# Two-input work leaves GpSimd, and due times come from the last order: a transformer of two layers and a mixed-attention block on one core

## The chip, the core and the metric

The kernel runs on one core of a Trainium2 chip, in one launch. The time is the device time of an execution in microseconds (us); the time before is the median of three executions.

The engines and their names in the rows: PE is TensorE (matrix products and transposes; PEld its weight loads), DVE is VectorE, ACT is ScalarE, POOL is GpSimd, SP is the engine that issues the DMAs. Each engine works off its own queue in the order in which the program was written out, and waits on semaphores for the others.

## The reference

512 rows of x (1024 wide), one vector c, batch 1, all in float32. Two layers, then a second block:

```python
c_act = jax.nn.silu(c)
for layer in range(2):
    mod = c_act @ ada_w[layer] + ada_b[layer]
    sh1, sc1, g1, sh2, sc2, g2 = jnp.split(mod, 6, axis=-1)
    h = modulate(rms_norm(x, norm_g[layer, 0]), sh1, sc1)      # h * (1 + sc1) + sh1
    y = gmlp_mixer(h, ...) if layer == 0 else nsa_mixer(h, ...)
    x = x + g1[:, None, :] * rms_norm(y, norm_g[layer, 1])
    h = modulate(rms_norm(x, norm_g[layer, 2]), sh2, sc2)
    y = jnp.square(jax.nn.relu(h @ ff_w_in[layer])) @ ff_w_out[layer]
    x = x + g2[:, None, :] * rms_norm(y, norm_g[layer, 3])

def gmlp_mixer(h, w_in, ln_g, ln_b, w_s, b_s, w_out):
    u, v = jnp.split(jax.nn.gelu(h @ w_in), 2, axis=-1)
    v = layer_norm(v, ln_g, ln_b)        # then 8 groups of 128 columns, chunks of 128 rows
    mixed = jnp.einsum('gts,bcsgd->bctgd', tril(w_s), v) + b_s
    return (u * mixed) @ w_out
```

nsa_mixer is an attention of 16 heads over compressed, selected and windowed keys; the second block is a sum of stick-breaking and differential attention with a gate, and an output product.

## The kernel before

Every product is done in three products of halves: a float32 tile is split into a rounded upper half and the rest (hi and lo, in names h and l at the end), and TensorE adds hi x hi, hi x lo and lo x hi. So each weight tile (raw, 128 rows of 1024 columns, straight from a DMA) needs a copy that rounds (wh, or twh in the tail of a product) and a subtraction (wl or twl = raw - wh), and activations need the same (ah and al, tah and tal, hh and hl, vh and vl, pth and ptl, ...). `split` puts the subtraction on VectorE; `splitw` lets the planner choose for both parts; `flex` lets it choose VectorE or GpSimd for any two-input instruction.

The program isn't written in the order in which it runs. A recorder (`Rec`) notes every operation with its engine, or a list of engines, its dependences and buffers. `once` is a list scheduler: with a cost for each instruction it places operation after operation on the engine that comes free first, by priority among those that are ready, and gives buffers of limited pools (raw has 4). `dates` then goes through that order backwards, works out by when each operation is due, and makes this the priority of the operations off TensorE in the next pass; TensorE's operations keep the order of the program as their priority. `order` does this up to 12 times, keeps the pass whose planned end is the earliest, and the instructions go out in that order. All are issued from one line (L615), so the rows below are told apart by tile names.

The stages in time: the mixer of layer 1 (`gmlp`: transposes tp of the normed x, named hx before and xT after; v = vps, 30 to 79 us; u = fmps, 79 to 125; the group products pm; the output product acc, 139 to 205), its feed-forward (from 205 us), keys and values and the attention of layer 2 (inside 594 to 874 us, sA, sB, sC, tA to tC, po), its feed-forward, and the second block (inside 1310 to 1564 us).

The start: `cc` is c, then its silu, computed by way of e = exp(-c), a reciprocal and a product. Eight small diagonal tiles `diag` of it go into a product of TensorE (`cbp`) that spreads c over the partitions as the row `cb`. The modulation vectors are dot products on VectorE of the rows of ada_w with cb (written raw<-raw,cb), each with a vector from memory (vcol) added, as B and S; xT is scaled and shifted by B and S and split into hh and hl before vps can start. The reciprocal roots of x are made from squares on ScalarE (junkx), hv, rt and xrs.

The tail of the mixer: mx is made from pm, sg = sg * mx is u * mixed, tah and tal are its halves, and acc takes them with twh and twl, the halves of a_w_out, one slice k of 128 rows after the other.

Of the kernel before, what the change touches and what calls it, by code (L numbers as in the profile page):

```python
# [26 lines left out]
F32 = mybir.dt.float32  # L27
# [194 lines left out]
class Rec:  # L222
# [157 lines left out]
    def dates(self):  # L380

        heirs, last = {}, {}
        for o in self.ops:
            for b in o.bufs:
                if b.res and id(b) not in heirs:
                    heirs[id(b)] = None
                    k = b.pool, b.slot
                    if k in last:
                        heirs[last[k]] = o
                    last[k] = id(b)  # L390
        due, nxt = {}, None
        for o in reversed(self.ops):
            e, d = o.eng[0], o.eng[4]
            t = 1e12 if nxt is None else nxt if e == "pe" else 1e12
            for x in o.succ:
                t = min(t, due[x] - LAT[e][x.eng[0]])
            for b in o.bufs:
                h = heirs.get(id(b))
                if h is not None and h is not o:
                    t = min(t, due.get(h, 1e12) - 200)  # L400
            if o.eng[1] == "dma_start":
                d += 2460
            due[o] = t - d
            if e == "pe":
                nxt = due[o]
            else:
                o.prio = due[o]
# [263 lines left out]
class KB:  # L671
# [52 lines left out]
    def splitw(self, hi, lo, src):  # L724

        self.copyw(hi, src)
        self.flex("tensor_sub", lo, src, hi.bitcast(F32))

    def copyw(self, dst, src):

# [2 lines left out]

    def flex(self, m, *a, **k):

        self.R.add([("dve", m, a, k), ("pool", m, a, k)])

    def mac(self, out, x, s, y):

# [1336 lines left out]
```

## Time and profile before

| | |
|---|---|
| median of 3 executions | 1586.44 us (1580.53 to 1587.76) |
| the profiled execution | 1586.38 us |
| its span, first to last instruction | 1584.6 us |
| mean granted TensorE clock | 0.984 of full speed |
| busy share PE, DVE, ACT, POOL | 95%, 70%, 42%, 27% |
| HBM read, written | 205.33 MB, 6.34 MB |

How to read it: an engine's busy time counts its instructions from start to end, and what it stands still within an instruction is in it. A wait of TensorE is put down to the instruction of another engine that ended last before it. The granted clock is the share of TensorE's full speed that it was given in a stretch.

### The profile page before, as it was taken

How to read it: one execution, taken by the hardware profiler on the slowest of the kernel's cores; microseconds unless marked ns; L12 is line 12 of the kernel's file. 1: busy time of each engine (PE TensorE's matmuls, PEld its weight loads, DVE VectorE, ACT ScalarE, POOL GpSimd, SP SyncE). 2: the span in 40 equal slices, each digit the busy share in tenths (PEclk: the TensorE clock that was granted, in tenths of full speed). 3: DMA queues.
4: the chain of work that ended last, by engine and by line, in shares of the span. 5: the costliest groups of instructions: out<-in, count | busy, mean ns of one | idle time of the engine just before them, and what ended most of it. 6: DMA issues, size and time to landing. Idle time of an engine off the chain costs nothing. (4 is left out here: it accounts for less than half of the span.)

```text
span 1584.6 us, 20197 instructions
## 1 busy us (share of the span) xinstructions
PE 1508.1 (95%) x7410; PEld 1256.2 (79%) x7410; DVE 1103.8 (70%) x1957; ACT 667.5 (42%) x1443; POOL 425.7 (27%) x415
## 2 busy tenths in 40 slices
PE   4997899999999999999998999999999999999988
PEld 3786788888888889787876898888888888878777
DVE  6897686567874478777886684555674568688882
ACT  4441342222121456577786332222111337667680
POOL 4044100000111131475676000000242024243560
PEclk9998899999999999999998999999999999999999
DMA  9756189537841071300115256538512251112312
GB/s 347 238 186 173 30 292 288 187 133 276 340 154 40 28 249 54 112 1 28 28 31 170 67 200 182 172 111 252 180 45 67 89 181 54 54 54 55 80 47 100
DMA packets 151395, 212.98 MB, mean 134 GB/s; under 512 B 49536, under 2 KB 110208, under 8 KB 151296
## 3 DMA queue, kind: packets, MB, share of 16 engines
q1 hardware_dynamic: 151296, 211.69, 41.7%
q8 instruction: 58, 0.95, 0.3%
q14 instruction: 41, 0.34, 0.1%
HBM read 205.33 MB, written 6.34 MB: 134 GB/s over the span
## 5 line engine op out<-in xcount | busy, mean ns | idle before, releaser
L615 DVE TENSOR_TENSOR wl<-raw,wh 128x1024 fp32r<-128x1024 f32 x176 | 230.9, 1315 | 55.7 <-PE fmps L615 18.5
L615 DVE CAST wh<-raw 128x1024 fp32r<-128x1024 f32 x118 | 88.7, 752 | 123.5 <-PE fmps L615 96.7
L615 PE MATMUL acc<-wh,ah 128*128 128x512 f32 x432 | 168.9, 392 | 0.0
L615 PE MATMUL acc<-wl,ah 128*128 128x512 f32 x432 | 168.6, 392 | 0.0
L615 DVE SCALAR_TENSOR_TENSOR raw<-raw,cb 128x1024 f32<-128x1024 f32 x112 | 146.4, 1329 | 6.7 <-DMA raw<-in_kv_ada_w_dram 6.0
L615 PE MATMUL acc<-wh,al 128*128 128x512 f32 x432 | 134.5, 391 | 0.0
L615 ACT ACTIVATE r<-fmps 128x512 f32<-128x512 f32 x64 | 38.4, 599 | 210.7 <-PE fmps L615 210.7
L615 POOL TENSOR_TENSOR al<-hid,ah 128x512 fp32r<-128x512 f32 x10 | 16.9, 1694 | 401.2 <-ACT ah L615 388.8
L615 PE MATMUL acc<-twh,tah 128*128 128x512 f32 x272 | 107.2, 402 | 3.3 <-DVE twh L615 3.3
L615 PE MATMUL acc<-twl,tah 128*128 128x512 f32 x272 | 107.3, 403 | 3.1 <-DVE twl L615 3.1
L615 PE MATMUL fmps<-hfh,wl 128*128 128x512 f32 (+1 forms) x288 | 106.0, 368 | 2.3 <-DVE wl L615 2.3
L615 PE MATMUL fmps<-hfl,wh 128*128 128x512 f32 (+1 forms) x288 | 105.6, 367 | 0.0
L615 PE MATMUL fmps<-hfh,wh 128*128 128x512 f32 (+1 forms) x288 | 105.4, 368 | 0.1
L615 PE MATMUL fmps<-hf1l,wh 128*128 128x512 f32 (+1 forms) x288 | 105.2, 366 | 0.0
L615 PE MATMUL fmps<-hf1h,wl 128*128 128x512 f32 (+1 forms) x288 | 105.2, 366 | 0.0
L615 PE MATMUL fmps<-hf1h,wh 128*128 128x512 f32 (+1 forms) x288 | 104.8, 365 | 0.0
L615 ACT CAST ah<-hid 128x512 fp32r<-128x512 f32 x47 | 29.1, 619 | 157.7 <-PE acc L615 157.7
L615 PEld LDWEIGHTS acc<-wl,ah 128*128 128x128 f32 x432 | 81.6, 189 | 16.9
L615 PEld LDWEIGHTS acc<-wh,ah 128*128 128x128 f32 x432 | 81.4, 189 | 16.8
L615 PEld LDWEIGHTS acc<-wh,al 128*128 128x128 f32 x432 | 81.4, 189 | 16.7
L615 PE MATMUL acc<-twh,tal 128*128 128x512 f32 x272 | 88.2, 400 | 3.2 <-DVE tal L615 3.2
L615 ACT CAST wh<-raw 128x1024 fp32r<-128x1024 f32 x57 | 59.3, 1049 | 55.9 <-PE fmps L615 25.7
(561 smaller groups left out, 3995.0 us busy)
## 6 DMA issues: line engine op xcount, KB each, us to landing
raw<-in_ada_w_dram SPq DMA_DIRECT2D x40, 1024.0 KB, 7.5
raw<-in_ff_w_in_dram SPq DMA_DIRECT2D x32, 1024.0 KB, 10.5
raw<-in_ff_w_out_dram SPq DMA_DIRECT2D x32, 1024.0 KB, 5.0
raw<-in_w_in_dram SPq DMA_DIRECT2D x16, 1024.0 KB, 5.6
raw<-in_w_ada_dram SPq DMA_DIRECT2D x12, 1024.0 KB, 11.1
raw<-in_a_w_in_dram SPq DMA_DIRECT2D x8, 1024.0 KB, 8.6
raw<-in_ada_w_dram SPq DMA_DIRECT2D x16, 512.0 KB, 11.9
raw<-in_kv_ada_w_dram SPq DMA_DIRECT2D x8, 1024.0 KB, 14.2
```

Of the source, the lines that this page charges most:

```text
L615: getattr(real[e], m)(*a, **k)
```

## The change

Three lines. `dates` took as due time of a product that of the next product (nxt), from the end of the program backwards; now it takes the product's own end in the last order, its start plus its cost (the cost comes off again two lines on, so the product is due when it started). `splitw` no longer leaves the subtraction to the planner, and `flex` has VectorE alone as its engine. `copyw` (a copy on ScalarE, VectorE or GpSimd) stays, as do the instructions that are written for GpSimd (ws * tril, cP, cr, some copies).

```diff
--- before.py
+++ after.py
@@ -391,7 +391,7 @@
         due, nxt = {}, None
         for o in reversed(self.ops):
             e, d = o.eng[0], o.eng[4]
-            t = 1e12 if nxt is None else nxt if e == "pe" else 1e12
+            t = o.start + d if e == "pe" else 1e12
             for x in o.succ:
                 t = min(t, due[x] - LAT[e][x.eng[0]])
             for b in o.bufs:
@@ -724,7 +724,7 @@
     def splitw(self, hi, lo, src):
 
         self.copyw(hi, src)
-        self.flex("tensor_sub", lo, src, hi.bitcast(F32))
+        self.dve.tensor_sub(lo, src, hi.bitcast(F32))
 
     def copyw(self, dst, src):
 
@@ -733,7 +733,7 @@
 
     def flex(self, m, *a, **k):
 
-        self.R.add([("dve", m, a, k), ("pool", m, a, k)])
+        self.R.add([("dve", m, a, k)])
 
     def mac(self, out, x, s, y):
```

What it does to the order, first on SP, at the very start of the program, where x_79 and the like are the four row blocks of x. SP before:

```order
L615 DMA x_79<-in_x_dram 128x1024
L615 DMA x_87<-in_x_dram 128x1024
L615 DMA x_92<-in_x_dram 128x1024
L615 DMA x_94<-in_x_dram 128x1024
L615 DMA cc<-in_c_dram 128x8x1
L615 DMA raw<-in_a_w_in_dram 128x2x1024
L615 DMA raw_100<-in_ada_w_dram 128x1024 x2
```

The vector c is the fifth here, and the weights a_w_in come ahead of ada_w. SP after:

```order
L615 DMA cc<-in_c_dram 128x8x1
L615 DMA x_87<-in_x_dram 128x1024
L615 DMA x_92<-in_x_dram 128x1024
L615 DMA x_94<-in_x_dram 128x1024
L615 DMA x_96<-in_x_dram 128x1024
L615 DMA raw_98<-in_ada_w_dram 128x1024 x2
L615 DMA raw<-in_a_w_in_dram 128x2x1024
```

c is issued first now instead of fifth, and two rows of ada_w stand before the first weights.

The second place is VectorE just after the constants, up to the first dots. VectorE before:

```order
L615 TENSOR_SCALAR hv<-ss 128x4
L615 TENSOR_SCALAR e<-e 128x8
L615 RECIPROCAL e<-e 128x8
L615 TENSOR_TENSOR rt<-xrs 128x4
L615 TENSOR_TENSOR cc<-cc,e 128x8
L615 TENSOR_TENSOR rt<-rt,hv 128x4
L615 TENSOR_SCALAR diag<-ident,cc 128x128 x8
L615 SCALAR_TENSOR_TENSOR xrs<-rt,xrs 128x4
L615 TENSOR_SCALAR hx<-x_87,xrs 128x512
L615 COPY cb<-cbp 128x512
L615 SCALAR_TENSOR_TENSOR raw_100,S_186<-raw_100,cb 128x1024
L615 SCALAR_TENSOR_TENSOR raw_100,B_215<-raw_100,cb 128x1024
```

The roots (hv, rt) stand between the steps of cc here, and hv waits for all four squares of x. VectorE after:

```order
L615 TENSOR_SCALAR e<-e 128x8
L615 RECIPROCAL e<-e 128x8
L615 TENSOR_TENSOR cc<-cc,e 128x8
L615 TENSOR_SCALAR diag<-ident,cc 128x128 x8
L615 COPY cb<-cbp 128x512 x2
L615 TENSOR_SCALAR hv<-ss 128x4
L615 SCALAR_TENSOR_TENSOR raw_98,B_150<-raw_98,cb 128x1024
L615 TENSOR_TENSOR rt<-xrs 128x4
L615 TENSOR_TENSOR rt<-rt,hv 128x4
L615 SCALAR_TENSOR_TENSOR xrs<-rt,xrs 128x4
L615 TENSOR_SCALAR hx<-x_92,xrs 128x512
L615 TENSOR_SCALAR hx<-x_96,xrs 128x512
```

The eight diag and the two copies of cb stand ahead of all of the roots (hv, rt, xrs) now. ScalarE moves likewise: e comes ahead of the four squares junkx and not behind them, and a second load of its function table between them is gone.

The third place is the tail of the mixer, from pm to acc. GpSimd before:

```order
L615 TENSOR_TENSOR tal<-sg_722,tah 128x512
L615 TENSOR_TENSOR sg_722<-sg_722,mx 128x512 x2
L615 TENSOR_TENSOR tal<-sg_722,tah 128x512
L615 TENSOR_SCALAR twh<-raw 128x1024
L615 TENSOR_TENSOR sg_928<-sg_928,mx 128x512
L615 TENSOR_TENSOR twl<-raw,twh 128x1024
L615 TENSOR_SCALAR twh<-raw 128x1024
L615 TENSOR_TENSOR tal<-sg_722,tah 128x512
L615 TENSOR_TENSOR sg_928<-sg_928,mx 128x512
L615 TENSOR_TENSOR tal<-sg_928,tah 128x512
L615 TENSOR_TENSOR twl<-raw,twh 128x1024
```

GpSimd has two-input instructions of three kinds here (tal, sg, twl); after, only copies (twh) are left there. VectorE before:

```order
L615 TENSOR_TENSOR twl<-raw,twh 128x1024
L615 SCALAR_TENSOR_TENSOR mx<-pm,lngb,E 128x512
L615 TENSOR_TENSOR sg_722<-sg_722,mx 128x512
L615 TENSOR_TENSOR twl<-raw,twh 128x1024
L615 SCALAR_TENSOR_TENSOR raw,S_1000<-raw,cb 128x1024
L615 TENSOR_TENSOR tal<-sg_722,tah 128x512
L615 SCALAR_TENSOR_TENSOR raw,S_1000<-raw,cb 128x1024
L615 TENSOR_TENSOR twl<-raw,twh 128x1024
L615 TENSOR_TENSOR S_1000<-S_1000,vcol 128x8
L615 SCALAR_TENSOR_TENSOR raw,B_834<-raw,cb 128x1024
L615 TENSOR_TENSOR sg_928<-sg_928,mx 128x512
L615 SCALAR_TENSOR_TENSOR raw,B_834<-raw,cb 128x1024
```

Four dots (raw<-raw,cb) stand among the twl, tal and sg. VectorE after, from the fourth twl on:

```order
L615 TENSOR_TENSOR twl<-raw,twh 128x1024
L615 SCALAR_TENSOR_TENSOR mx<-pm,lngb,E 128x512
L615 TENSOR_TENSOR tal<-sg_711,tah 128x512
L615 TENSOR_TENSOR sg_711<-sg_711,mx 128x512
L615 TENSOR_TENSOR twl<-raw,twh 128x1024
L615 TENSOR_TENSOR tal<-sg_711,tah 128x512
L615 SCALAR_TENSOR_TENSOR mx<-pm,lngb,E 128x512
L615 TENSOR_TENSOR sg_931<-sg_931,mx 128x512
L615 TENSOR_TENSOR twl<-raw,twh 128x1024
```

The twl, tal and sg that GpSimd had stand on VectorE now, one mx, tal, sg and twl after the other, and the dots come ahead of this place or behind it, but for one.

## Rows read from the trace of the kernel before

**Rows 1.** Page, part 1: busy us (share of the span) xinstructions of each engine

```profile
PE 1508.1 (95%) x7410; PEld 1256.2 (79%) x7410; DVE 1103.8 (70%) x1957; ACT 667.5 (42%) x1443; POOL 425.7 (27%) x415
```

**Rows 2.** Busy time by stretches (window, length, engines with instructions, clock, DMA share, GB/s)

```profile
30.00:79.00 49.00, 47.09 (x193) 38.21 (x193) 40.02 (x77) 19.35 (x32) 6.20 (x4) 0.93 0.82 273
139.00:160.00 21.00, 14.32 (x39) 10.20 (x40) 21.00 (x20) 6.95 (x10) 15.42 (x8) 0.67 0.34 118
160.00:205.00 45.00, 40.00 (x179) 32.65 (x178) 32.76 (x59) 16.35 (x41) 7.47 (x3) 0.92 0.32 77
240.00:540.00 300.00, 300.00 (x1330) 248.48 (x1329) 189.02 (x258) 69.28 (x115) 25.65 (x19) 1.00 0.54 189
594.00:874.00 280.00, 264.38 (x1507) 217.93 (x1507) 219.68 (x543) 192.00 (x483) 157.21 (x205) 0.98 0.22 60
1310.00:1564.00 254.00, 239.10 (x1212) 200.61 (x1211) 198.91 (x352) 164.32 (x369) 110.01 (x93) 0.99 0.20 58
```

**Rows 3.** TensorE's waits, whole run: us in total, times, longest us

```profile
PE cbp L615 <- DVE diag L615: 18.1, 1, 18.1
...
PE acc L615 <- DVE twh L615: 3.3, 1, 3.3
```

**Rows 4.** Timelines of four engines, 4 to 30 us: start us, us, instruction

```profile
4.42 1.06 ACT L615 ACTIVATE junkx<-x 128x1024 f32<-128x1024 f32 x1 [2.40 <-DMA x<-in_x_dram]
...
11.28 0.21 ACT L615 ACTIVATE e<-cc 128x8 f32<-128x8 f32 x1
...
12.99 5.85 DVE L615 TENSOR_SCALAR diag<-ident,cc 128x128 f32<-128x128 f32 x8
...
13.14 4.64 POOL L615 TENSOR_TENSOR wl<-raw,wh 128x1024 fp32r<-128x1024 f32 x2
...
29.73 1.12 PE L615 MATMUL vps<-wh,hh 128*128 128x512 f32 x2 [2.59 <-ACT hh L615]
```

**Rows 5.** Tile cc: durations ns min/median/max of the diag made from it

```profile
L615 DVE TENSOR_SCALAR diag<-ident,cc x8: 273/275/2380, 13.0 to 18.6; 128x128 f32<-128x128 f32 x8
```

**Rows 6.** Timelines of VectorE, GpSimd and TensorE, 138 to 206 us

```profile
138.57 0.69 DVE L615 CAST twh<-raw 128x1024 fp32r<-128x1024 f32 x1 [5.72 <-DMA raw<-in_a_w_out_dram]
...
146.33 3.41 DVE L615 SCALAR_TENSOR_TENSOR raw<-raw,cb 128x1024 f32<-128x1024 f32 x1
...
156.70 1.21 DVE L615 SCALAR_TENSOR_TENSOR raw<-raw,cb 128x1024 f32<-128x1024 f32 x1
...
159.59 0.68 DVE L615 TENSOR_TENSOR tal<-sg,tah 128x512 fp32r<-128x512 f32 x1
...
145.29 3.37 POOL L615 TENSOR_TENSOR twl<-raw,twh 128x1024 fp32r<-128x1024 f32 x1
...
205.12 0.28 PE L615 MATMUL fmps<-hfh,wh 128*128 128x256 f32 x1
```

**Rows 7.** VectorE's groups from 139 to 160 us: xcount, busy us, mean ns

```profile
L615 DVE SCALAR_TENSOR_TENSOR raw<-raw,cb 128x1024 f32<-128x1024 f32 x4 | 8.1, 2035 | 0.0
L615 DVE TENSOR_TENSOR twl<-raw,twh 128x1024 fp32r<-128x1024 f32 x3 | 6.6, 2215 | 0.0
L615 DVE TENSOR_TENSOR tal<-sg,tah 128x512 fp32r<-128x512 f32 x2 | 2.2, 1095 | 0.0
```

**Rows 8.** GpSimd's groups, whole run

```profile
L615 POOL TENSOR_TENSOR wl<-raw,wh 128x1024 fp32r<-128x1024 f32 x18 | 46.6, 2589 | 17.1 <-DVE wh L615 11.1 <-PE dpo L615 2.2 <-issue 2.1
...
L615 POOL TENSOR_TENSOR al<-hid,ah 128x512 fp32r<-128x512 f32 x10 | 16.9, 1694 | 401.2 <-ACT ah L615 388.8 <-PE acc L615 7.8 <-DVE ah L615 4.7
```

**Rows 9.** VectorE's groups, whole run

```profile
L615 DVE TENSOR_TENSOR tal<-hid,tah 128x512 fp32r<-128x512 f32 x7 | 11.2, 1624 | 0.0
```

**Rows 10.** GpSimd's wl from 0 to 240, 594 to 874, 1310 to 1564 us

```profile
L615 POOL TENSOR_TENSOR wl<-raw,wh 128x1024 fp32r<-128x1024 f32 x5 | 13.5, 2700 | 8.7 <-DVE wh L615 8.6
...
L615 POOL TENSOR_TENSOR wl<-raw,wh 128x1024 fp32r<-128x1024 f32 x3 | 8.0, 2663 | 5.6 <-DVE wh L615 2.5 <-issue 2.1 <-PE po L615 1.0
...
L615 POOL TENSOR_TENSOR wl<-raw,wh 128x1024 fp32r<-128x1024 f32 x9 | 21.8, 2418 | 2.8 <-PE dpo L615 2.2 <-ACT wh L615 0.2
```

## The prediction

> **What bounds the kernel now.** I read the page first, then busy time by stretches, then TensorE's waits, then the timelines of the places that came out of these. On the page [rows 1] TensorE is busy 1508.1 of 1584.6 us; VectorE has 70%, GpSimd 27%. So the work on TensorE is the floor, and only the stretches where it runs dry can give anything.
>
> The stretches [rows 2] say which these are. From 240 to 540 us TensorE is busy 300.00 of 300 us with 1330 instructions at a granted clock of 1.00, which is 300/1330 = 0.226 us for each. I use that as the price of a 512-column product without a wait. There, and in the other feed-forward, work that VectorE gains or loses lies under products: VectorE has 189 of the 300 us. Losses stand in four places. (1) The first product starts at 18.11 us; its wait is the longest of the kernel [rows 3]. (2) From 139 to 160 us only 39 products run in 21 us (39 x 0.226 = 8.8, so 12.2 lost), VectorE is busy in all 21.00 us, the granted clock is 0.67 (between the two levels of 1.2 and 2.4 GHz), and from 160 to 205 another 45 - 179 x 0.226 = 4.5 us go: 16.7 us together, and the waits of acc for twh [rows 3] and for other split halves are in it. (3) From 594 to 874 us (the attention of layer 2) TensorE is idle 280 - 264.4 = 15.6 us. (4) From 1310 to 1564 us 254 - 239.1 = 14.9 us.
>
> What makes place 1 late [rows 4]: the sigmoid of c stands on ScalarE behind four squares of x and a second table load, so e starts at 11.28 us. Then VectorE has eight diag, 275 ns at the median; the longest takes 2380 ns [rows 5], and the eight 5.85 us, while GpSimd works on two wl from 13.14 us on. They end at 12.99 + 5.85 = 18.8 instead of 12.99 + 8 x 0.275 = 15.2. The reciprocal roots and, through the column cb, the first product of the mixer (vps, 29.73 us) wait behind that.
>
> What makes place 2 late [rows 6]: beside GpSimd's twl of 3.37 us VectorE's dot takes 3.41 us; alone, ten us later, the same form takes 1.21, and a tal 0.68.
>
> **The price of a two-input instruction.** GpSimd takes 2589 ns on a mean for a wl of 128x1024 [rows 8], where VectorE alone takes 1.21 us for that size; at 128x512 it is 1694 against 0.68. And GpSimd's time isn't free for VectorE: the seven tal that it does now among GpSimd's work take 1624 ns on a mean [rows 9]. VectorE's 139 to 160 us by groups [rows 7] give 4 x (2035 - 1210) + 3 x (2215 - 1210) + 2 x (1095 - 680) = 7.1 us, and with two small ones 8.5 us, above the undisturbed times. The same subtraction over VectorE's rows of a stretch gives some 40 us before 240 us, 13 in place 3 and 41 in place 4.
>
> The Trainium skill ("SBUF — State Buffer", section "SBUF: two separate sides") has VectorE and GpSimd share a port pair that the first one holds for its whole instruction while the other stands still. The 2380 ns of a 275 ns diag agree. The same notes ("Perfetto Trace Analysis", section "Optimizing Scalar/DVE Operations") speak on the other side as well: with VectorE saturated, giving work to ScalarE or even GpSimd may make sense. By that advice the stretches where VectorE is fullest would become slower; rival C works that out from rows, and the durations just given are why I think less of it.
>
> **Edit by edit.** Edits two and three (splitw, flex) give all these instructions to VectorE. GpSimd keeps one-input copies, which still disturb, the mask products and cP, cr; its instructions fall from 420 to 342, VectorE's rise by 102 (the order's counts). By stretch, from the counts on GpSimd (its wl in each stretch: [rows 10]) and VectorE's undisturbed durations:
>
> - To 222 us: 5 wl and 2 twl at 1.21, 5 vg, 5 sg, 4 tal, 3 vl at 0.68: 8.5 + 11.6 = +20 us. Against it stand the 40 us of delay; I let 8 of them stay, for copies. VectorE's net: -12.
> - Place 3: 3 wl, 3 twl, 8 instructions of 128x512, 4 ptc of 0.41 us: 7.3 + 5.4 + 1.6 = +14. Of 13 us of delay perhaps 10 go. Net +4; TensorE is dry there in 6% of the time and VectorE busy 78%, so about half shows: **+2** (bounds -6, no delay left and the shorter latencies shown, and +14, all work shown and no delay gone).
> - Place 4: 9 wl, 2 twl, 16 of 128x512, 9 smaller: 13.3 + 10.9 + 3.7 = +28; of 41 us of delay some 35 go. Net -7, half of it shown: **-4** (bounds -15, all the idle time, and +12).
> - The feed-forwards take the rest (6 of 128x1024, 19 al and tal: 7.3 + 12.9 = 20 us) and hide it under saturated products: 0. Were that cover gone, these 20 us would show.
>
> Edit one (the due time of a product is now its own start in the last order, with no chain backwards without gaps) costs no instruction. It reorders, and three things of it can be seen in the order. SP issues c first, before x. ScalarE does e before the squares, with one table load. VectorE does the diag before the roots. So place 1: c takes the place in which x landed by 4.42 us (start of the first square, [rows 4]); from e's start to the first diag there are 12.99 - 11.28 = 1.7 us, with two instructions of the roots between, and 8 x 0.275 = 2.2 us follow: diag ends at 4.4 + 1.7 + 2.2 = 8.3 us, and 3 us later if c should land that much after x did. From the first product to vps the trace has 29.73 - 18.11 = 11.6 us; I keep it, though the vector vcol and the first ada rows have to land too: vps at 20 to 22 us. **-9** (bounds -4, if the landings hold it, and -10).
>
> Then 30 to 79 us: 193 x 0.226 = 43.6 of 49 us; VectorE 40.02 busy. What edits two and three add here is about what they take away; 0. From there to 125 us the products run without a gap, and the +3.4 of vg and +2 of vl stand against some 7 us of delay; 0.
>
> Place 2: GpSimd's twl, tal and sg become 2 x 1.21 + 4 x 0.68 + 5 x 0.68 = 8.5 us on VectorE, and the 8.5 us of delay above and some 5 more up to 170 us go. The order helps more: of the four dots among the twl only one is left there, the others (3 x 1.21, now 2.04 each) come behind. VectorE then has mx, sg, tal and twl of 0.74 + 0.68 + 0.68 + 1.21 = 3.3 us for each slice k, TensorE 24 products of 0.226 = 5.4. So after the first slice it can keep ahead, and the waits shrink to the first. I take **-9** of the 16.7 (bounds -2 and -14; a start below the full clock stays).
>
> **The sum**: -9 - 9 + 2 - 4 = -20 us. The profiled run took 1586.38 us (span 1584.6), as good as the median of 1586.44, so: **1566 us**.
>
> **Rivals.**
> - A, the head start does not last: the weights of a_w_out land late. VectorE's twh waited 5.72 us for that landing [rows 6]. If buffers come free no sooner, -9 of place 1 shrinks to -2, and place 2 gives the half: -2 - 4 + 2 - 4 = 1578. For it: the DMA engines are 0.82 busy from 30 to 79 us; against it: 0.34 from 139 to 160 [rows 2].
> - B, no change to speak of: the delay by GpSimd's two-input instructions is only moved to its copies, which the new order makes more of (twh 7 to 13, pth and ptc too), and the new due times hold the old gaps: place 1 alone gains, and +14 of place 3 meets it: -9 + 9 = 1586.
> - C, VectorE becomes the bound, on the other side: in place 3, where it is 78% busy on the mean, heads run in a chain of mask, exponential, split and product, and every added instruction that stands ahead of a ptl delays TensorE. It decides if VectorE passes about 90% from 680 to 840 us; then +14 and place 4's +12 show, less 10 for the start: 1602.
> - D, the delays matter more than I counted: places 3 and 4 lose all their excess, -6 and -15, and the first stage -23: 1542.
>
> **Chances.** Forecast 0.52, A 0.16, B 0.11, C 0.11, D 0.10. Half a per cent is 8 us, about what a measurement of this kernel can tell from no change; the lines are 1578.5 and 1594. Faster: all of the forecast but 0.02, half of A, all of D: 0.68, and 0.04 from B; 0.72. Slower: C and a little of B, 0.11; the rest, 0.17, is the same. The range drops the ends of C and D: 1548 to 1588; the forecast's own is 1556 to 1577.
>
> **What would show it.** GpSimd has no wl, twl, al or tal; the first product stands at 8 to 11 us and vps at 20 to 22; no diag is above 0.4 us; from 139 us on no dot takes over 2 us, and acc's waits fall below 3 us together; the first layer's feed-forward (fmps from hfh) begins near 187 instead of 205.12 us [rows 6]; VectorE's count rises by 102 and its busy time by less than the 20 + 14 + 28 + 20 = 82 us that were given to it. I am wrong if vps is not earlier than 26 us, if TensorE's busy share falls in 680 to 840 us, or if copies on GpSimd delay VectorE as much as wl did.

## The result, and the profile after

The changed kernel takes 1558.47 us on the median of four executions (1554.99 to 1562.43), beside 1585.66 us of the kernel before (1580.53 to 1587.76): a ratio of 0.9834, interval 0.980 to 0.987. In a second set of runs it was 0.9808 (0.9795 to 0.9821), 30 us less. The forecast was 1566 us, 20 less than before, and a range of 1548 to 1588. The profiled execution took 1554.99 us with a span of 1553.2 us, 31 us less than the profile before; it was the fastest of the four, so the differences by stage below add up to a few us more than the medians give (31 against 27).

The page of the changed kernel, busy time by engine, to hold against [rows 1]:

```profile
PE 1499.9 (97%) x7410; PEld 1252.3 (81%) x7410; DVE 1086.9 (70%) x2059; ACT 651.0 (42%) x1419; POOL 261.7 (17%) x337
```

TensorE's busy share is 97% instead of 95%. It stands still for 53.3 us (1553.2 - 1499.9) where it stood still for 76.5, and its 7410 instructions are busy for 8.2 us less. So 23 of the 31 us are waits, and 8 are the same products in less time; the granted clock below bears on those. VectorE has 2059 instructions instead of 1957, the 102 that the order said, and is busy 17 us *less* (1086.9 against 1103.8), though it took over work of 82 us. GpSimd fell by 164 us.

TensorE's longest waits, whole run (us in total, times, longest), to hold against [rows 3]:

```profile
PE tp L615 <- DVE rt L615: 7.3, 1, 7.3
PE cbp L615 <- DVE diag L615: 4.8, 1, 4.8
PE wst L615 <- POOL ws L615: 4.7, 1, 4.7
PE tp L615 <- ACT hx L615: 4.6, 1, 4.6
PE fmps L615 <- ACT vg L615: 4.4, 1, 4.4
```

The 18.1 us in front of cbp are 4.8. The waits of acc, 9.6 us together before, have left one of 0.7. Two of these five are new, wst and fmps, both before the mixer's group products; they are spoken of below.

The diag, to hold against [rows 5], and tal beside its row of before [rows 9], both on VectorE:

```profile
L615 DVE TENSOR_SCALAR diag<-ident,cc x8: 281/281/288, 3.9 to 5.3; 128x128 f32<-128x128 f32 x8
```

```profile
L615 DVE TENSOR_TENSOR tal<-hid,tah 128x512 fp32r<-128x512 f32 x16 | 12.4, 814 | 0.0
```

No diag is held up any more (288 ns at the most against 2380), and sixteen tal take 814 ns on a mean where seven took 1624.

Some of TensorE's instructions on its timeline (start us, us), at fixed points of the first 125 us, with the wait in brackets:

```profile
4.85 2.07 PE L615 MATMUL cbp<-diag,shared 128*128 128x512 f32 x2 [4.85 <-DVE diag L615]
...
19.31 0.71 PE L615 MATMUL vps<-wh,hh 128*128 128x512 f32 x2
...
67.69 0.79 PE L615 MATMUL fmps<-hh,wh 128*128 128x512 f32 x1 [4.40 <-ACT vg L615]
...
88.43 1.12 PE L615 MATMUL wst<-ident,ws 128*128 128x128 f32 x4 [4.66 <-POOL ws L615]
...
122.46 0.33 PE L615 MATMUL pm<-wsT,vh 128*128 128x128 f32 x2
```

The first product is at 4.85 us, vps at 19.31 instead of 29.73 [rows 4]: 10.4 us earlier. But pm starts at 122.46, and before at 125.3: of the 10.4 us only 2.8 are left there, lost at the waits of 63.3 to 67.7 and of 83.8 to 88.4.

Stretches of the changed kernel (columns as in [rows 2]):

```profile
20.00:40.00 20.00, 20.00 (x89) 16.12 (x88) 19.78 (x40) 8.72 (x11) 1.07 (x1) 1.00 1.02 410
60.00:80.00 20.00, 15.60 (x60) 12.41 (x59) 14.91 (x45) 13.29 (x35) 2.13 (x2) 0.83 1.02 327
80.00:100.00 20.00, 15.34 (x63) 12.28 (x62) 9.86 (x32) 6.73 (x11) 3.59 (x3) 0.83 0.84 198
133.00:154.00 21.00, 20.26 (x89) 15.89 (x89) 20.26 (x27) 6.38 (x9) 3.67 (x3) 1.00 0.27 101
154.00:190.00 36.00, 28.71 (x130) 23.81 (x129) 24.78 (x60) 13.96 (x37) 1.55 (x1) 0.91 0.42 103
240.00:520.00 280.00, 280.00 (x1241) 231.95 (x1240) 178.46 (x251) 59.68 (x100) 8.55 (x8) 1.00 0.53 191
576.00:849.00 273.00, 261.01 (x1505) 216.26 (x1504) 226.06 (x562) 191.04 (x482) 129.33 (x190) 0.98 0.23 62
1285.00:1533.00 248.00, 239.20 (x1213) 201.03 (x1212) 194.50 (x383) 159.63 (x359) 67.38 (x76) 0.99 0.19 59
```

From 20 to 40 us the DMA engines are full (1.02). After the two waits the granted clock is 0.83 in both stretches, where products without a wait have 1.00; a part of each loss is a product at the lower of the two levels. In the tail of the mixer, now 133 to 154, 89 products run in 21 us where 39 did, at a clock of 1.00, and the half after it is shorter. The windows of the attention and of the second block are set so that they hold the same products as in [rows 2] within two (1505 and 1507, 1213 and 1212): 273 us instead of 280, and 248 instead of 254. From 240 to 520 us nothing shows: 1241 instructions in 280 us, 0.226 us each, as before.

The places at which an instruction starts, in the traces, and the lead on the kernel before:

| | before | changed | lead |
|---|---|---|---|
| first product (cbp) | 18.1 | 4.8 | 13.3 |
| first vps | 29.7 | 19.3 | 10.4 |
| first pm | 125.3 | 122.5 | 2.8 |
| eighth hfl (VectorE; all transposes for the first feed-forward done) | 222.5 | 202.6 | 20.0 |
| R (VectorE; keys and values of layer 2) | 594.3 | 576.1 | 18.2 |
| first hf1l (VectorE; attention done) | 897.1 | 872.3 | 24.7 |
| eighth h2l (VectorE; second block begins) | 1281.5 | 1255.4 | 26.1 |
| last fy (VectorE) | 1581.1 | 1549.7 | 31.4 |

The first product of the feed-forward (fmps from hfh) starts at 190.58 us, before at 205.12.

The second profiled execution of the same kernel runs within 0.6 us of the first up to 771 us and is 4.1 us behind by 853. The attention, from R to the first hf1l, in the kernel before, the changed kernel and its second profile (columns as in [rows 2]):

```profile
594.27:897.07 302.80, 287.18 (x1611) 236.81 (x1610) 230.37 (x563) 197.40 (x498) 157.21 (x205) 0.98 0.21 59
576.12:872.33 296.21, 284.22 (x1611) 235.53 (x1610) 235.58 (x581) 195.81 (x496) 129.33 (x190) 0.98 0.22 60
576.67:876.43 299.76, 288.31 (x1611) 238.60 (x1610) 236.01 (x580) 195.93 (x496) 129.32 (x190) 0.97 0.22 60
```

TensorE stands still for 15.6 us before and for 12.0 and 11.5 us in the two profiles after. The second of these is longer although it waits less: the same 1611 instructions are busy for 4.1 us more, at a granted clock of 0.97 instead of 0.98. So a length in the attention is known to about 4 us only, its waits much better.

### The profile page after: what moved, and what is told of

Same layout as the page of the kernel before. It is cut to its first block, busy times and chain, and to the rows that moved or that the text cites. A ratio compares the mean times of both kernels' runs of the same rounds, so it can differ in the third digit from the quotient of the medians.

```text
span 1553.2 us, 20146 instructions
## 1 busy us (share of the span) xinstructions
PE 1499.9 (97%) x7410; PEld 1252.3 (81%) x7410; DVE 1086.9 (70%) x2059; ACT 651.0 (42%) x1419; POOL 261.7 (17%) x337
## 3 DMA queue, kind: packets, MB, share of 16 engines
HBM read 205.33 MB, written 6.34 MB: 136 GB/s over the span
## 4 chain that ended last, share of the span: by engine, by line
PE 79%; DVE 11%; ACT 3%; DMA 3%; issue 2%; POOL 1%; SPq 1%; POOLq 0%; DVEq 0%; ACTq 0%
PE acc L615 29%; PE fmps L615 27%; PE tmc L615 3%; PE qps L615 3%; PE po L615 3%; PE sgps L615 2%; DVE wl L615 2%; DVE raw L615 1%; PE vps L615 1%; PE tmb L615 1%; PE sB L615 1%; DVE ptl L615 1%; PE tp L615 1%; PE sA L615 1%; PE kps L615 1%
## 5 line engine op out<-in xcount | busy, mean ns | idle before, releaser
L615 DVE TENSOR_TENSOR wl<-raw,wh 128x1024 fp32r<-128x1024 f32 x194 | 239.4, 1236 | 39.4 <-PE fmps L615 18.5
L615 DVE CAST wh<-raw 128x1024 fp32r<-128x1024 f32 x119 | 83.6, 703 | 120.3 <-PE fmps L615 94.3
L615 DVE SCALAR_TENSOR_TENSOR raw<-raw,cb 128x1024 f32<-128x1024 f32 x112 | 133.9, 1222 | 11.9 <-DMA raw<-in_kv_ada_w_dram 7.2
L615 ACT CAST ah<-hid 128x512 fp32r<-128x512 f32 x48 | 29.7, 620 | 159.4 <-PE acc L615 159.4
L615 POOL TENSOR_SCALAR tah<-hid 128x512 fp32r<-128x512 f32 x5 | 5.3, 1076 | 472.5 <-DMA raw<-in_ff_w_out_dram 208.5
L615 ACT CAST wh<-raw 128x1024 fp32r<-128x1024 f32 x52 | 54.5, 1049 | 55.2 <-PE fmps L615 32.0
## 6 DMA issues: line engine op xcount, KB each, us to landing
raw<-in_ff_w_in_dram SPq DMA_DIRECT2D x32, 1024.0 KB, 10.4
raw<-in_w_ada_dram SPq DMA_DIRECT2D x12, 1024.0 KB, 11.8
```

The costliest lines, as they stand in the source:

```text
L615: getattr(real[e], m)(*a, **k)
```

## The experiments

"VectorE's delay" below is a sum over its instructions in a trace: what each one took beyond the lower quartile of the times of its operation and shape in that trace, where it took more. For the kernel before it is 36 us before 240 us, 14 from 594 to 874 and 40 from 1310 to 1564; for the changed kernel 9, 7 and 13 in the same windows. Over the whole run 129 became 43.

Where these delays lie says who makes them. In the kernel before 142 instructions are held up by over 0.1 us, 116 us together, and every one of them overlaps an instruction on GpSimd: 87 a two-input one (96.5 us), 55 one-input ones alone (19.8 us). In the changed kernel it is 29 us in 78 instructions, and 76 of them (28.8 us) overlap one-input instructions alone.

**The due times alone.**

```diff
-            t = 1e12 if nxt is None else nxt if e == "pe" else 1e12
+            t = o.start + d if e == "pe" else 1e12
```

> The kernel before with the due-time line alone; VectorE and GpSimd share the two-input work as before, by a new plan. Theory of the forecast (the port between VectorE and GpSimd costs most, the due times only bring c and the diag ahead): the first product near 5 us and vps near 20, but the tail of the mixer and the attention stay as slow as before, so about 1586 - 10 = 1576 us (0.994). Rival (the better order does it all, the engine matters little): about 1558, as the full change. Second rival (the start's gain is caught by the next wait): 1582 to 1586.

Measured: 1577.06 us, 0.9938 (0.9914 to 0.9962). The total is the one that the theory of the forecast gave, and the first rival falls. The stages are not as the theory had them: vps has a lead of 9.9 us and pm of 4.4, so half of it is caught by the next waits; the tail (8.2 at the eighth hfl), which was to stay as slow as before, gains 3.8 us in the new plan, the attention 3.1 (6.4 at R, 9.4 at the first hf1l), and the end has 11.6. That the sum fits is in part luck. The tal among GpSimd's work are as slow as in [rows 9]:

```profile
L615 DVE TENSOR_TENSOR tal<-hid,tah 128x512 fp32r<-128x512 f32 x8 | 11.9, 1507 | 0.0
```

**The engines alone.**

```diff
-        self.flex("tensor_sub", lo, src, hi.bitcast(F32))
+        self.dve.tensor_sub(lo, src, hi.bitcast(F32))
...
-        self.R.add([("dve", m, a, k), ("pool", m, a, k)])
+        self.R.add([("dve", m, a, k)])
```

> The kernel before with the two engine edits alone, due times as before. Theory of the forecast: the start stays late (c behind x, first product at about 16, since no wl delays a diag), the tail of the mixer, the attention and the second block gain what the port gave back: 1586 - 17 = 1569 us (0.989). Rival (the order does it all): 1586. If both edits are needed for each other, both single runs stay above 1575.

Measured: 1554.41 us, 0.9787 (0.9765 to 0.9809). More than forecast, and all that the full change gives. c is late here as in the kernel before (first product at 13.8, vps at 23.3, a lead of 6.4), pm is at 125.5 with no lead at all, and yet the eighth hfl has 17.2 us and the end 30.7. So the early c is not needed for the gain.

**The same order, other engine.**

```diff
+        for o in self.ops:
+            if o.eng[0] == "pool" and len(o.alts) == 2 and o.alts[0][1] == o.alts[1][1]:
+                o.eng = o.alts[0]
         self.ops.sort(key=lambda o: (o.start, o.seq))
```

> The order of the kernel before, row for row, but every two-input instruction that the plan gave to GpSimd is issued on VectorE at its place in that order. Nothing else moves. If the port is the cause, the change of engine alone gains even in an order that was not made for it: 1586 - 12 = 1574 us, most of it before 240 us and after 1310. If it is the work on VectorE that counts and the gain comes of the new order, this is slower than before: 82 us more work in a plan that has no room for it, 1590 to 1600.

Measured: 1575.24 us, 0.9921 (0.9902 to 0.994). The change of engine alone gains 12.6 us in an order that wasn't made for it; the engines with an order made for them (1554.41 in the same set) gain 20.8 more. Where the 12.6 lie is the more telling part: the lead is 5.5 us at vps, 7.3 at pm, 10.9 at the eighth hfl and at R, 4.5 at hf1l, and 10.7 at the end. In the second block this kernel gains 6.2 us. The attention is 6.4 us longer (columns as in [rows 2]):

```profile
583.35:892.57 309.22, 293.40 (x1611) 241.32 (x1610) 237.29 (x581) 198.11 (x498) 126.42 (x187) 0.96 0.21 58
```

But TensorE doesn't wait more there, 15.8 us against 15.6 before: its products are busy for 6.2 us more, at a granted clock of 0.96 instead of 0.98. The added work doesn't show as waits even in this order. The clock alone moves this stretch by 4 us between two executions of one kernel, so whether the order has a part in the 6.4 us stays open.

From pm to the first product of the feed-forward (fmps from hfh) the kernel before, this run and the changed kernel take:

```profile
125.25:205.12 79.87, 65.28 (x314) 53.62 (x312) 59.62 (x86) 24.97 (x53) 26.66 (x14) 0.87 0.43 112
117.98:195.69 77.71, 64.15 (x314) 52.70 (x313) 57.73 (x100) 24.95 (x53) 2.15 (x2) 0.89 0.44 114
122.46:190.58 68.12, 60.09 (x314) 50.70 (x312) 54.09 (x97) 22.62 (x50) 7.07 (x5) 0.95 0.38 114
```

The engine alone gains 2.2 us here and the changed kernel 11.8; the engines alone with their own order gain 12.4 (67.5 us). In this place the planner's new order, made for the engines, does the larger part.

**ws on VectorE too.**

```diff
-            self.pool.tensor_mul(w, w, self.tril[:, None, :].to_broadcast([128, 4, 128]))
+            self.dve.tensor_mul(w, w, self.tril[:, None, :].to_broadcast([128, 4, 128]))
```

> The changed kernel with one more two-input product, ws * tril (two instructions), on VectorE. In the changed kernel TensorE waits 4.7 us for GpSimd's ws at 83 us, and what the start had gained has shrunk from 10.4 us (vps) to 2.8 us (pm). If that wait is what takes the start's gain, pm comes 4 to 5 us earlier and the time is about 1554 (0.980 of before). Rival: the mixer's middle is bound by VectorE and the landing of weights, and another wait takes its place: 1558, as the changed kernel.

Measured: 1550.2 us, 0.9762 (0.974 to 0.9783), the lowest ratio of all runs (the run without copies, below, is level with it), but not for the reason expected. The wait stays, with another engine's name on it:

```profile
PE wst L615 <- DVE ws L615: 4.5, 1, 4.5
```

pm comes 1.1 us earlier, and the eighth hfl at 202.8 has gained nothing. Its profile ends 5.6 us ahead of the changed kernel's: 2.0 of it lie in the attention, which is known to 4 us only, and 3.6 in the second block, which the planner put into another order (the lead grows from 28.1 us at h2l to 37.0 at the end). That GpSimd's ws was the cause of the wait falls.

**The changed kernel again, and ws with the old due times.** The first is the changed kernel as it stands; the second is the kernel before with the engine edits and ws on VectorE.

> The changed kernel itself once more, beside the kernels of this call, because the engine edits alone gave 0.979 and the full change 0.983 in another call. If the new due times cost something beside the engine edits, this comes out at 0.983 again, some 5 us behind the engine edits alone; if that was the spread between calls, 0.979 to 0.981.

> The engine edits and ws * tril on VectorE, with the old due times (c late at the start). With the new due times the same gave 0.976. If the new due times add nothing to the engine edits, 0.976 here too; if the start's 4 us (vps at 19 against 23) are worth something once ws is off GpSimd, this is 3 to 4 us slower, 0.978 to 0.979; if they cost, it is 0.972.

Measured: 1555.61 us, 0.9808 (0.9795 to 0.9821), and 1553.92 us, 0.9803 (0.979 to 0.9816). The first is the second guess: sets of runs differ by 0.3%. In one set the two kernels agree, but they differ in ws as well. Taken by pairs, with ws on VectorE the new due times are 0.4% better (0.9762 against 0.9803), and with ws on GpSimd 0.2 to 0.5% worse (0.9808 and 0.9834 against 0.9787), each time from different sets. With the engine edits in, these runs can't tell the sign of what the new due times are worth.

**Work given back, stage by stage.** Three kernels issue the order of the changed kernel row for row, but in one part of the program every n-th of the two-input instructions that the change bound to VectorE goes to GpSimd at its place; a fourth does so in the mixer.

```diff
+        c = [o for o in self.ops if o.bk and o.stage == "nsa"]
+        for i in range(18):
+            o = c[(2 * i + 1) * len(c) // 36]
+            o.eng = o.bk
```

> The order of the changed kernel, row for row, but in the keys, values and attention of layer 2 every n-th two-input instruction, 18 in all, goes to GpSimd at its place in the order. My forecast had this stretch 2 us slower by the change; the trace shows it 6.5 us faster. If the port between the two engines makes that gain, the 18 cost 4 to 10 us against the changed kernel (0.986 to 0.990). If the work on VectorE counted, they give 1 to 3 us (0.981 or less); if the gain came from the new order alone, nothing.

> The same with 19 two-input instructions of the mixer of layer 1, as many as the plan before had there. The port: 8 to 17 us slower than the changed kernel (0.989 to 0.994), with the loss between 120 and 200 us and on the way to vps. The new order: 0 to 3 us.

> The order of the changed kernel, row for row, but in the two feed-forwards every n-th two-input instruction, 36 in all, goes to GpSimd at its place. The forecast had these under saturated products, whichever engine does them: the time of the changed kernel within 2 us (0.981 to 0.983), though VectorE's delay grows by 30 us or more. If the port costs wherever it is used, 5 to 15 us slower.

> The same in the second block, 28 instructions to GpSimd. The forecast gave this stretch 4 us of gain, the trace shows 6 to 7. The port: 5 to 9 us slower than the changed kernel (0.984 to 0.988), VectorE's delay there back from 13 us towards 41. The new order: 0 to 2 us.

Measured, with the changed kernel at 0.9808 and 0.9834 in its two sets (the first two runs stand in the set of 0.9808; the last two, and the two experiments after them, in a set without it):

| given back | ratio (interval) | VectorE's delay in its window, changed kernel to this |
|---|---|---|
| 18 in the attention | 0.9844 (0.9829 to 0.9858) | 7 to 16 us |
| 19 in the mixer | 0.9843 (0.9829 to 0.9856) | 9 to 29 us |
| 36 in the feed-forwards | 0.9866 (0.985 to 0.9882) | 43 to 83 us (whole run) |
| 28 in the second block | 0.9899 (0.9884 to 0.9914) | 13 to 28 us |

The first two are 5.6 and 5.0 us slower than the changed kernel, the attention inside the expected 4 to 10 us, the mixer below its 8 to 17. (In the attention itself, from R to the first hf1l, the lead grows by 1.1 us with the 18 given back, where the changed kernel's two profiles have 6.6 and 3.0; TensorE stands still for 14.6 us there, against 12.0 and 11.5.) Most of the mixer's delay is back, and the eighth hfl comes 4.7 us later than in the changed kernel, so a quarter of the lead of 20.0 there is lost; the order is still that of the changed kernel. Its tail (columns as in [rows 2]) has 78 products where 89 ran and before 39:

```profile
133.00:154.00 21.00, 17.89 (x78) 13.61 (x77) 18.29 (x19) 5.97 (x8) 15.11 (x8) 1.00 0.27 101
```

With 28 given back in the second block the kernel loses 10 to 14 us by the ratios. In the trace the block takes 303.2 us from the eighth h2l to the last fy, where the changed kernel takes 294.3 and the kernel before took 299.6: 8.9 us, the upper end of what was expected (the ratio is above it), and more than the change had gained there. Of the 8.9, 5.6 are waits (15.4 us against 9.8). An order that doesn't reckon with GpSimd pays more for it than one that does.

For the feed-forwards the time is that of the second guess (5 to 9 us by the ratios), but nearly everywhere in them the products ran on as if nothing had happened, under 40 us more of delay on VectorE:

```profile
240.00:520.00 280.00, 280.00 (x1241) 231.91 (x1241) 184.58 (x237) 60.06 (x100) 45.23 (x23) 1.00 0.53 190
1000.00:1180.00 180.00, 180.00 (x796) 149.05 (x795) 109.42 (x127) 39.88 (x62) 33.68 (x17) 1.00 0.44 153
```

One place gave way, the seam between the attention and the second feed-forward, where TensorE isn't covered (GpSimd, VectorE and TensorE on their timelines):

```profile
888.12 2.38 POOL L619 TENSOR_TENSOR wl<-raw,wh 128x1024 fp32r<-128x1024 f32 x1 [46.95 <-DVE rt L619]
890.47 1.49 POOL L619 TENSOR_SCALAR wh<-raw 128x1024 fp32r<-128x1024 f32 x1
...
879.70 1.41 DVE L619 SCALAR_TENSOR_TENSOR hx<-hx,xr,S4w 128x512 f32<-128x512 f32 x2
...
888.24 4.26 DVE L619 SCALAR_TENSOR_TENSOR hx<-hx,xr,S4w 128x512 f32<-128x512 f32 x2
...
891.19 0.63 PE L619 MATMUL tp<-ident,hx 128*128 128x128 f32 x4 [1.26 <-DVE hx L619]
```

Two hx take 1.41 us at 879.70 and 4.26 at 888.24: the first of these 2.81, beside a wl of 2.38 us on GpSimd, the second 1.53, beside a copy wh of 1.49. hx is what the transposes wait for, and the lead falls from 23.6 at the first hf1l to 19.9 at the last. The time lost by this kernel by the ratios is more than these 3.7 us. Its profile, the fastest of its four executions, ends 4.8 and 0.6 us behind the two of the changed kernel; the rest I could not place.

**Five raw buffers.**

```diff
-RAW, WT = 4, 4
+RAW, WT = 5, 4
```

> The changed kernel with five buffers for raw weights instead of four. In it vps begins 10.4 us earlier than before and pm only 2.8 us. If the head start is lost because DMAs are issued late, behind buffers that are not free, the wait for ws at 83 us and the one at 63 us shrink, pm comes 4 us earlier or more, and the time is some 4 us less (0.978). If the DMA engines are full and the bytes themselves are late, pm stays within 1.5 us and so does the time.

Measured: 1556.74 us, 0.9822 (0.9807 to 0.9837). Half of each guess: the wait for ws is gone, and pm comes 5.4 us earlier than in the changed kernel, so that load was late because of buffers. The wait for vg at 63 us stays (4.1 us against 4.4), so buffers are not shown to be its cause. The time is the same, since TensorE comes to wait at the next landing (timelines of TensorE and ScalarE):

```profile
117.02 0.33 PE L615 MATMUL pm<-wsT,vh 128*128 128x128 f32 x2
...
128.96 1.04 ACT L615 CAST twh<-raw 128x1024 fp32r<-128x1024 f32 x1 [6.34 <-DMA raw<-in_a_w_out_dram]
...
130.06 0.73 PE L615 MATMUL acc<-twh,tah 128*128 128x512 f32 x2 [2.21 <-ACT twh L615]
```

ScalarE waits 6.34 us for a_w_out, acc for ScalarE's twh, and at the eighth hfl this kernel (205.1) is 2.6 us behind the changed one. From pm to there it takes 8.0 us longer; 2.5 of them are waits, and the granted clock is 0.92 against 0.96.

**Copies off GpSimd too.**

```diff
         self.R.add([("act", "copy", (dst, src), {}), ("dve", "tensor_copy", (dst, src), {}),
-                    ("pool", "tensor_scalar", (dst, src, 1.0, 1.0), dict(op0=OP.mult, op1=OP.mult))])
+                    ])
```

> The changed kernel with the rounding copies (wh, twh, tah and the like) on ScalarE or VectorE only, so that they leave GpSimd too. VectorE's instructions still take 69 us more than undisturbed in the changed kernel. If the one-input copies on GpSimd cause a good part of it, that falls below 45 us and the time by 3 to 8 us (0.977 to 0.980). If they cost little and GpSimd's help is worth having, the copies now on VectorE and ScalarE cost: 2 to 8 us slower.

Measured: 1549.8 us, 0.9769 (0.9737 to 0.98). VectorE's delay falls from 43 to 23 us by the count above (the 69 of the expectation is by another) and the time by some 6 to 10 us against the changed kernel's two ratios. It loses 3.6 us up to the eighth hfl and gains 10.3 from h2l to the end more than the changed kernel did (15.6 against 5.3); there TensorE stands still for 3.8 us instead of 9.8. So the planner does better without GpSimd's copies. How much of that is the delay and how much the new order isn't shown: no run takes the copies off GpSimd in an unchanged order.

## Why the prediction was right, step by step

The direction, the range and the main cause held. The parts of the sum -9 - 9 + 2 - 4 came out differently, and that the sum fits is in part luck: in the profile the start gives 6 us less than its term by pm, and the attention 5 to 9 us more than its own (two profiles).

**The start, -9.** vps moved by 10.4 us, for the reasons given: c first (it landed by 3.04 us, when e began, not 4.4), e before the squares, the diag undisturbed. The step after it failed: "30 to 79" and "79 to 125" at 0 each. They take 7.6 of the 10.4 us back. From vps to pm TensorE stands still for 9.1 us, where it stood still for 2.5. In the changed kernel's chain of waits, two pieces between 40 and 100 us are DMAs, and ScalarE, whose vg is waited for at 63 us, has a wh and a table load in front of it:

```profile
60.67 8.04 DMA raw<-in_ada_w_dram
...
75.87 11.10 DMA ws<-in_a_w_s_dram
...
64.60 1.04 ACT L615 CAST wh<-raw 128x1024 fp32r<-128x1024 f32 x1 [11.13 <-DMA raw<-in_a_w_in_dram]
65.66 1.28 ACT L615 ACT_TABLE_LOAD   x1
```

That wh waited 11.13 us for a_w_in. This is the mechanism of rival A, one stage earlier than I put it; the run with five buffers shows that the wait for ws comes of buffers and that a_w_out is next in line, where A had it. A head start need not be lost, though: in the order of before with the other engine it is 5.5 us at vps and 7.3 at pm, with 2.9 us of waits between. The loss goes with the new order: there the first ws is issued at 75.9 us and lands at 87.0, in the order of before with the other engine it is issued at 77.2 and in use at 80.05. As a part of the whole change the new due times, on which the start rests, add nothing that these runs can tell; alone they give 10.8 us.

**The tail of the mixer, -9.** Right in kind and nearly in size: the prediction's place 2 ends where the feed-forward begins, and from pm to there 79.9 us became 68.1, -11.8. (Up to the eighth hfl it is 97.3 to 80.1, but 19 products that ran before it now run after it, some 4.3 us at 0.226.) The delay of the groups went as worked out (columns as in [rows 7], from 133 to 154 us):

```profile
L615 DVE TENSOR_TENSOR twl<-raw,twh 128x1024 fp32r<-128x1024 f32 x6 | 7.3, 1216 | 1.3 <-ACT twh L615 1.3
L615 DVE TENSOR_TENSOR tal<-sg,tah 128x512 fp32r<-128x512 f32 x6 | 5.1, 851 | 0.0
L615 DVE SCALAR_TENSOR_TENSOR raw<-raw,cb 128x1024 f32<-128x1024 f32 x2 | 2.4, 1212 | 0.0
```

twl has 1216 ns where it had 2215, a dot 1212 where it had 2035. The waits fell by 6.6 us (14.6 to 8.0). The other 5.2 are the same 314 instructions in less time: the granted clock is 0.95 instead of 0.87, and 1.00 instead of 0.67 in the stretch that was the worst. The prediction named the clock there and let its part stay. The engine alone in the old order gives 2.2 of these 11.8 us and an order made for it the rest; the due times have no part in it (-12.4 without them).

**The attention, +2.** The sign was wrong: -6.6 in the profile, -3.0 in the second profile of the same kernel. The step that failed is "half shows", said of +14 of work less 10 of delay. None of it shows as a wait, in either order: TensorE stands still for 15.8 us with the work moved in the old order, 15.6 before, and 12.0 and 11.5 in the order that the planner made, with due times or without (11.8 for the engines alone). The rest of each difference is the same 1611 instructions in more or less time, at another granted clock. Rival C was this sum at its bound, and its condition didn't come: from 680 to 840 us VectorE is busy 135.6 of 160 us, 85%.

**The second block, -4.** -5.3 and -5.1 from h2l to the last fy in the two profiles, -6.2 in the old order. Nearly the term.

**The feed-forwards, 0.** They hold: 280.00 of 280 us with the moved work on VectorE, and also with 36 instructions on GpSimd, more than the 25 that the plan before had there. The seams were not on my list: from the first product of the first feed-forward to R the lead grows by 3.6 us.

**Signs and sums.** The first product came at 4.85 us, earlier than the 8 to 11 of the prediction, and the feed-forward at 190.6, not near 187. One sign of being wrong did come: TensorE's busy share in 680 to 840 us fell, from 152.2 to 150.5 of 160 us. But by then the changed kernel is 18 us ahead, so the window holds other work; over the 1611 instructions from R to hf1l the share rose from 94.8% to 96.0%. Rival B's sum has +9 where its text has the +14 of place 3; with 14 it is 1591.

**The cause.** That work on GpSimd makes this kernel slower is shown by the runs that only change the engine, both ways, in the old order and in the new one. That this work holds VectorE up is shown by the delays, which overlap GpSimd's instructions, all but one. These runs change GpSimd's own longer time (2589 ns for a wl where VectorE takes 1.21 us) together with the delay, so they don't divide the loss between the two. What TensorE waited for says something of it: in the kernel before 56.4 us of its waits end with an instruction of VectorE and 5.4 with one of GpSimd, in the changed kernel 21.3 and 10.8. With work given back, TensorE waits 3.4 us in the attention and 4.0 in the second block for a wl or a ptl that GpSimd now makes, so there a good part may be GpSimd's own time; in the mixer such waits are 0.2 us.

The Trainium skill's rule on the shared pair ("SBUF — State Buffer", section "SBUF: two separate sides") agrees with the first hx of 2.81 us, which starts 0.12 us after the wl and ends 0.54 us after it. Of what the Trainium skill says in "Perfetto Trace Analysis", section "Optimizing Scalar/DVE Operations", the prediction gave one half, that work from a full VectorE may go to GpSimd; the other half is that the two share a read port, so that moving work between them might not help. The trace agrees with the second: a twl on VectorE takes 1216 ns from 133 to 154 us, with GpSimd busy for 3.67 of the 21 us, and took 2215 before, with GpSimd busy for 15.42 of 21.

## What to carry to other kernels

An instruction on GpSimd has two prices, its own time and the time for which it stops VectorE; add both before calling it free, and look for instructions of VectorE that take twice their usual time. Under products without a wait neither shows, at the seams between stages both do. Where a planner writes the order, don't add up an edit on the order of before: the new order was worth more here than the change of engine in the old one (20.8 us against 12.6), and in it a lead at the start lasted only up to the next load that had not landed. And look at waits and granted clock apart before a difference of a stage is put down to an edit.

## What was not expected of the hardware

That one-input copies on GpSimd would still disturb VectorE stood in the prediction; that one-input instructions make nearly all of the delay that is left did not. With the copies gone it fell by another 20 us, and the time, in another order, by 0.4 to 0.7%. And the copies are slower beside VectorE in turn. A wh of 128x1024 on GpSimd took 1.04 us at 64.69 us in the changed kernel, with VectorE idle; on a mean, with none of the planner's two-input work left on GpSimd, it is (groups of GpSimd, whole run, mean ns):

```profile
L615 POOL TENSOR_SCALAR wh<-raw 128x1024 fp32r<-128x1024 f32 x23 | 29.2, 1273 | 226.5 <-DMA raw<-in_w_in_dram 70.4 <-PE acc L615 51.0 <-DMA raw<-in_a_w_in_dram 47.4
L615 POOL TENSOR_SCALAR twh<-raw 128x1024 fp32r<-128x1024 f32 x13 | 17.3, 1333 | 109.1 <-DMA raw<-in_ff_w_out_dram 28.1 <-DMA raw<-in_a_w_out_dram 27.4 <-DVE al L615 25.8
```
